# The second layer's down projection as seven products of sums of blocks, with tokens on the partitions, placed between the steps of the up projection

## The chip, the cores and the metric

The kernel runs on one core of one Trainium2 chip. The metric is the device time of one execution in microseconds. The kernel before was run three times: 2359.8, 2360.07 and 2360.8 us, a median of 2360.07 us. Engines are named as in the profile: PE multiplies matrices, PEld is its loading of weights, DVE, ACT and POOL work elementwise, SP issues most of the DMAs.

## What is computed

A decoder of two layers over 16 meta tokens and 256 tokens, with a residual stream of 2048 features, all in float32. The change touches the channel mixer of the second layer and the final norm behind it:

```python
def squared_relu_mlp(h, w_up, w_down):
    u = h @ w_up
    return jnp.square(jax.nn.relu(u)) @ w_down
...
        h = h + squared_relu_mlp(rms_norm(h, norm_mlp[layer]), w_up[layer], w_down[layer])
    return rms_norm(h, final_norm)[:, N_META:]
```

`w_up` is 2048 x 8192 and `w_down` 8192 x 2048 in each layer. The result has the 256 tokens alone, so in the second layer the meta tokens go into keys and values only.

## The kernel before

The residual `hT` lies with features on the partitions: 16 chunks of 128 features, 272 columns of tokens each. Every large product is a `gemm_group` (line 161): it computes 512 output features as four PSUM accumulators (`accs`) over 2048 input features, in four steps `kb` that each load 1 MB of weights (`raw`, line 185, on SP's queue, three buffers).

Products keep float32 precision by splitting each operand into two float32r parts: ACT writes the high part (`whi`, line 197), DVE subtracts it from the operand and so has the low part (`wlo`, line 198), in pieces of 128x1024. The activations are split likewise (`Split`, line 109). Three products make one: high by high, high by low, low by high. In the first layer they are three matmuls of 272 columns (lines 220 to 222). In the second layer (`pairs`) the first two are one matmul of 512 columns, since the high and low parts of 256 tokens lie side by side (line 217), and the third has 256 columns (line 218). The weights are the stationary operand, the activations the moving one.

`mlp` (line 444) goes over four quarters `f` of the 8192 hidden features: four groups of the up projection, whose results are scaled, rectified (lines 235 and 457), squared (line 459) and split (lines 460 and 461) into `u`, then four groups of the down projection, each adding its accumulators to `hT` (line 228). So in the second layer the stage has 1024 pairs of matmuls for the up projection and 1024 for the down projection. The final norm sums squares with small matmuls (line 594), takes the reciprocal root (lines 614 to 620), spreads it over the partitions (line 626) and scales and stores the result (lines 632 to 643).

PSUM has eight banks in two pools of four: `pacc` for the accumulators of `gemm_group` and `patt` for all else. The order of the instructions in each engine's queue is made by a planner, which estimates how long each one takes, from the order of the program; waits are put in by it too. In the kernel before POOL does little: masks at the start, small copies that pack keys, queries and values for the attention (lines 316 and 417), and two products at the end (line 641).

Of the kernel before, what the change touches and what calls it, by code (L numbers as in the profile page):

```python
# [15 lines left out]
P = 128  # L16
D = 2048
# [15 lines left out]
def yoco_kernel(ctx: ExitStack, tc: tile.TileContext, hT_in, gains, b_f, w_f, w_qkv0, w_o0, w_up, w_dn,  # L33
                w_kv, w_q1, w_o1, outT):
# [5 lines left out]
    align = ctx.enter_context(tc.tile_pool(name="align", bufs=1))  # L40
# [3 lines left out]
    att = ctx.enter_context(tc.tile_pool(name="att", bufs=2))  # L44
# [8 lines left out]
    bf_sb = const.tile([NC, 1], F32, name="bf_sb")  # L53
# [5 lines left out]
    for _ in range(7):  # L59
        nc.tensor.matmul(idle[:, :P], mean_w, mean_w, start=True, stop=True)  # L60
    ident = const.tile([P, P], F32, name="ident")
    make_identity(nc, ident)
    nones = const.tile([P, P], F32, name="nones")
    nc.vector.memset(nones, -1.0)
    nones_r = const.tile([P, P], F32R, name="nones_r")
    nc.vector.tensor_copy(nones_r, nones)

    ntri = const.tile([P, P], F32, name="ntri")
# [3 lines left out]
    ntri_r = const.tile([P, P], F32R, name="ntri_r")  # L72
# [3 lines left out]
    maskA = const.tile([P, 416], F32, name="maskA")  # L76
# [6 lines left out]
    maskM = const.tile([64, 4, 32], F32, name="maskM")  # L83
# [7 lines left out]
    maskB = const.tile([P, 400], F32, name="maskB")  # L91
# [6 lines left out]
    maskC = const.tile([64, 4, M], F32, name="maskC")  # L98
# [6 lines left out]
    pad = align.tile([P, 32], F32, name="pad")  # L105
# [55 lines left out]
    def gemm_group(wblk, sp, t0, evac, before={}, after={}, load_x=None, pairs=False, apart=()):  # L161
# [9 lines left out]
        for kb in range(4):  # L171
# [36 lines left out]
            for kc, m in order:  # L208
# [7 lines left out]
                if pairs and m not in apart:  # L216
# [6 lines left out]
                if last:  # L223
                    evac(m, [accs[m][:, :n]] + ([accs[m][:, n:]] if pairs and m not in apart else []))
# [34 lines left out]
    fq_sb = const.tile([P, 2, NC], F32, name="fq_sb")  # L259
    fqm_sb = const.tile([64, 4], F32, name="fqm_sb")  # L260
# [12 lines left out]
    def forget_gates(rstd):  # L273

        wf_hi, wf_lo = box["wf"]
        pf = patt.tile([P, 512], F32, tag="patt", name="pf")
        for k in range(NC):
            nc.tensor.matmul(pf[:NC, :T], wf_hi[:, k, :], xa.hi[:, k], start=k == 0, stop=False)
            nc.tensor.matmul(pf[:NC, :T], wf_hi[:, k, :], xa.lo[:, k], start=False, stop=False)
            nc.tensor.matmul(pf[:NC, :T], wf_lo[:, k, :], xa.hi[:, k], start=False, stop=k == NC - 1)  # L280
        fx = tmp.tile([P, T], F32, tag="relu", name="fx")[:NC]
# [43 lines left out]
    vz = const.tile([P, 4, P], F32, name="vz")  # L325
# [118 lines left out]
    def mlp(layer, xm, norm, t0, last_evac):  # L444
# [5 lines left out]
        for f in range(N_FF):  # L450
            u = Split(f"u{layer}_{f}", t0)
            for g in range(4):
                def evac(m, acc, g=g):
                    c = 4 * g + m
                    r = tmp.tile([P, T], F32, tag="relu", name=f"relu_{layer}_{f}_{c}")
                    u2 = tmp.tile([P, T], F32, tag="u2", name=f"u2_{layer}_{f}_{c}")
                    nc.vector.scalar_tensor_tensor(out=r[:, t0:], in0=total(acc, r[:, t0:]), scalar=0.0, in1=box["r"][:, t0:],
                                                   op0=ALU.max, op1=ALU.mult)
                    nc.scalar.activation(u2[:, t0:], r[:, t0:], AF.Square)
                    nc.scalar.activation(u.hi[:, c], u2[:, t0:], AF.Copy)  # L460
                    nc.vector.tensor_tensor(out=u.lo[:, c], in0=u2[:, t0:], in1=u.hi[:, c].bitcast(F32),
                                            op=ALU.subtract)
                gemm_group(w_up[layer, f, g], xm, t0, evac, {3: get_rstd} if f == g == 0 else {},
                           pairs=t0 == M)
            for g in range(4):
                def evac(m, acc, g=g):
                    residual_add(4 * g + m, acc, t0)
                    if f == N_FF - 1:
                        last_evac(4 * g + m)
                gemm_group(w_dn[layer, f, g], u, t0, evac, pairs=t0 == M,  # L470
                           apart=(3,) if layer == 1 and f == N_FF - 1 and g == 3 else ())
# [12 lines left out]
    mlp(0, xm, norm_m, 0, after_layer0)  # L484
# [104 lines left out]
    pms = patt.tile([P, 512], F32, tag="patt", name="pms_fin")  # L589
    box = {}  # L590

    def add_squares(src, first, last):
        for b in range(2):
            nc.tensor.matmul(pms[:, b:b + 1], src[:, M + b * P:M + (b + 1) * P], mean_w[:, 0:1],
                             start=first and b == 0, stop=last and b == 1)

    normf = Norm("fin", M)

    def last_evac(c):
        if c < NC - 4:  # L600
            normf.add(c)
        else:
            if c == NC - 4:
                add_squares(normf.acc, True, False)
            sq = tmp.tile([P, T], F32, tag="sq", name=f"sq_fin_{c}")
            nc.scalar.activation(sq[:, M:], hT[:, c, M:], AF.Square)
            add_squares(sq, False, c == NC - 1)
        if c < NC - 4:
            nc.scalar.activation(hT[:, c, M:], hT[:, c, M:], AF.Copy, scale=g_sb[:, G_FIN, c:c + 1])

    mlp(1, xm, norm_m, M, last_evac)
    fin = tmp.tile([P, 4, 2], F32, tag="fin", bufs=1, name="fin")
    a, y, t, rs = (fin[:, i, :] for i in range(4))
    nc.vector.tensor_scalar(a, pms[:, :2], EPS, None, op0=ALU.add)
# [80 lines left out]
```

## Time and profile before

| | |
|---|---|
| median of the runs | 2360.07 us |
| the profiled execution, its own time | 2360.31 us |
| its span (first to last instruction) | 2358.6 us |
| granted TensorE clock, mean | 0.998 |
| instructions | 39145 |
| bytes read from HBM over the span | 407.29 MB |
| DMA, mean rate over the span | 175 GB/s |

The span runs from the first instruction of the program to its last one; the execution's time holds 1.7 us more, which lie around it. An engine's busy time counts each moment once. A matmul's own duration is longer than the distance to the next one, because they are pipelined: what a matmul costs is read from how many start in a stretch of time. A DVE instruction too starts some 0.08 us before the one ahead of it has ended.

### The profile page before, as it was taken

The numbers are of one execution on the slowest core, as the hardware profiler recorded it, in microseconds if no ns is written. First come the engines' busy times: TensorE is split into PE (matmuls) and PEld (weight loads), VectorE is DVE, ScalarE is ACT, GpSimd is POOL, SyncE is SP. The second block draws the span as 40 slices with busy tenths as digits, with TensorE's granted clock in tenths as the row PEclk, the third lists the DMA queues.
The fourth block names the chain that finished last, engine by engine and source line by source line (L and its number), as shares of the span: only waits on it lengthen the run. The fifth ranks groups of instructions, "written<-read, shape, count | busy, mean of one in ns | idle before, by whom it ended". The sixth has DMA issues, their size and how long they took to land.

```text
span 2358.6 us, 39145 instructions
## 1 busy us (share of the span) xinstructions
PE 2344.8 (99%) x16512; PEld 2211.8 (94%) x16512; DVE 1343.1 (57%) x1916; ACT 1057.1 (45%) x1471; POOL 35.9 (2%) x64
## 2 busy tenths in 40 slices
PE   9999999999999999999999999999999999999998
PEld 9999999999999999999998999988888888888887
DVE  7565555655455455445566555566555655655665
ACT  5443344543344344344445444445543543543543
POOL 0000000000000000000000000000000000000000
PEclk9999999999999999999999999999999999999999
DMA  6444444554545455554545444445555555455453
GB/s 235 145 164 171 155 159 163 176 180 169 189 163 186 171 180 178 179 179 173 178 168 197 156 147 145 144 177 180 183 178 193 192 183 197 169 190 195 178 196 125
DMA packets 61039, 411.92 MB, mean 175 GB/s; under 512 B 7088, under 2 KB 10048, under 8 KB 12096
## 3 DMA queue, kind: packets, MB, share of 16 engines
q1 hardware_dynamic: 58976, 406.27, 48.5%
q8 instruction: 129, 2.11, 0.4%
q10 hardware_dynamic: 1888, 3.16, 0.4%
q14 instruction: 46, 0.38, 0.0%
HBM read 407.29 MB, written 2.11 MB: 174 GB/s over the span
## 4 chain that ended last, share of the span: by engine, by line
PE 99%; DVE 0%; ACT 0%; DMA 0%; issue 0%; DVEq 0%; SPq 0%; ACTq 0%
PE acc L217 25%; PE acc L220 19%; PE acc L221 19%; PE acc L222 19%; PE acc L218 13%; PE ps L365 0%; PE pza L542 0%; PE pv L307 0%; PE po L426 0%; PE po L427 0%; PE po L581 0%; PE po L582 0%; PE pzb L543 0%; PE po L428 0%; DMA g_sb<-gains 0%; ACT whi L197 0%
## 5 line engine op out<-in xcount | busy, mean ns | idle before, releaser
L198 DVE TENSOR_TENSOR wlo<-raw,whi 128x1024 fp32r<-128x1024 f32 (+1 forms) x771 | 932.5, 1220 | 761.5 <-ACT whi L197 758.2
L197 ACT ACTIVATE whi<-raw 128x1024 fp32r<-128x1024 f32 (+1 forms) x771 | 803.2, 1054 | 1072.4 <-PE acc L221 678.3
L217 PE MATMUL acc<-x_m,whi 128*128 128x512 f32 x1024 | 343.1, 394 | 0.5 <-DVE relu L235 0.5
L217 PE MATMUL acc<-x_u,whi 128*128 128x512 f32 x1008 | 337.9, 394 | 0.0
L220 PE MATMUL acc<-x_u,whi 128*128 128x272 f32 (+1 forms) x1040 | 297.7, 289 | 0.0
L221 PE MATMUL acc<-x_u,whi 128*128 128x272 f32 (+1 forms) x1040 | 294.8, 286 | 0.0
L220 PE MATMUL acc<-x_m,whi 128*128 128x272 f32 x1024 | 293.4, 289 | 0.0
L221 PE MATMUL acc<-x_m,whi 128*128 128x272 f32 x1024 | 290.4, 286 | 0.0
L222 PE MATMUL acc<-x_u,wlo 128*128 128x272 f32 (+1 forms) x1040 | 285.2, 284 | 0.0
L222 PE MATMUL acc<-x_m,wlo 128*128 128x272 f32 x1024 | 280.7, 284 | 0.0
L218 PE MATMUL acc<-x_m,wlo 128*128 128x256 f32 x1024 | 252.6, 282 | 0.0
L218 PE MATMUL acc<-x_u,wlo 128*128 128x256 f32 x1008 | 247.6, 281 | 0.0
L220 PE MATMUL acc<-x_a,whi 128*128 128x272 f32 x768 | 222.1, 294 | 0.7 <-ACT x_a L122 0.7
L221 PE MATMUL acc<-x_a,whi 128*128 128x272 f32 x768 | 221.0, 292 | 0.0
L217 PEld LDWEIGHTS acc<-x_m,whi 128*128 128x128 f32 x1024 | 185.0, 188 | 30.3 <-DVE relu L235 0.9
L222 PE MATMUL acc<-x_a,wlo 128*128 128x272 f32 x768 | 210.5, 287 | 0.0
L218 PEld LDWEIGHTS acc<-x_m,wlo 128*128 128x128 f32 x1024 | 192.3, 188 | 19.4 <-DVE wlo L198 4.6
L217 PEld LDWEIGHTS acc<-x_u,whi 128*128 128x128 f32 x1008 | 182.4, 188 | 29.7
L218 PEld LDWEIGHTS acc<-x_u,wlo 128*128 128x128 f32 x1008 | 189.3, 188 | 15.9 <-DVE wlo L198 1.6
L220 PEld LDWEIGHTS acc<-x_u,whi 128*128 128x128 f32 x1040 | 195.5, 188 | 0.2
L221 PEld LDWEIGHTS acc<-x_u,whi 128*128 128x128 f32 x1040 | 195.3, 188 | 0.1
L220 PEld LDWEIGHTS acc<-x_m,whi 128*128 128x128 f32 x1024 | 192.5, 188 | 0.0
(246 smaller groups left out, 3613.0 us busy)
## 6 DMA issues: line engine op xcount, KB each, us to landing
raw<-w_up SPq DMA_DIRECT2D x128, 1024.0 KB, 4.9
raw<-w_dn SPq DMA_DIRECT2D x128, 1024.0 KB, 4.9
raw<-w_qkv SPq DMA_DIRECT2D x45, 1024.0 KB, 4.8
raw<-w_o SPq DMA_DIRECT2D x32, 1024.0 KB, 4.8
raw<-w_kv SPq DMA_DIRECT2D x32, 1024.0 KB, 4.9
raw<-w_q SPq DMA_DIRECT2D x16, 1024.0 KB, 4.8
fk<-f_dram ACTq DMA_DIRECT2D x4, 544.0 KB, 5.2
raw<-w_qkv SPq DMA_DIRECT2D x4, 512.0 KB, 8.3
```

What stands on the lines that cost most here:

```text
L197: on_act = nc.scalar.activation(hp, src, AF.Copy)
L198: on_dve = nc.vector.tensor_tensor(out=lp, in0=src, in1=hp.bitcast(F32), op=ALU.subtract)
L217: nc.tensor.matmul(accs[m], wh, sp.both[:, k], start=first, stop=False)
L218: nc.tensor.matmul(accs[m][:, :n], wl, hi, start=False, stop=last)
L220: nc.tensor.matmul(accs[m][:, :n], wh, hi, start=first, stop=False)
L221: nc.tensor.matmul(accs[m][:, :n], wh, lo, start=False, stop=False)
L222: nc.tensor.matmul(accs[m][:, :n], wl, hi, start=False, stop=last)
```

## The change

The down projection of the second layer no longer goes through `gemm_group`. Tokens become the output's partitions: the result is held in `res`, 128 tokens by 2048 features for each half of the tokens, and the squared activations are now the stationary operand and the weights the moving one. `to_tokens` turns the residual round by 32 transposes, during the first block of the up projection.

The hidden features are taken in eight blocks `b` of 1024. For one block the activations are a matrix of 256 tokens by 1024 features, cut into 2x2 quarters, and so are the weights (512 features by 1024 outputs each quarter). The product of the two is computed by seven products of quarters or sums of quarters where the plain way takes eight. `build_forms` makes the seven forms of the activations for a block (four sums and the split of each, all on DVE and ACT). `down_block` goes over four pieces `n` of 256 columns of each half of the outputs, and over four steps `kp`: a step takes 128x256 of each quarter of the weights, makes four sums on POOL (`t`), splits three quarters and four sums on ACT and DVE (`hi`, `lo`: 128x768 and 128x1024), and issues 21 matmuls of 256 columns (`PRODUCTS`, three each) into the four banks of `patt`. After the fourth step the seven results are added to the four quarters of `res`, with two copies on ACT, five additions on DVE and six on POOL.

The weights are put into memory in this order on the host (`_quarters`), 1 MB for two steps. The steps of block b-1 are handed out behind the steps `kb` of the two up groups of block b by `SHARE`: none, 2, 2, 2, 2, 3, 3, 2. The last block runs by itself behind the last up group.

The final norm takes its sums of squares from ACT (`accum_out`) on `res`, the gain comes as a row spread over the partitions (`g_fin`), POOL multiplies three quarters of the last block's results by it, and the output goes out token by token. Smaller parts: the masks and other tiles of the attention move to a pool that is closed before the second layer's channel mixer; the matmuls ahead of the first load grow from 7 to 9; the products of the forget gates (`gate_products`) are issued ahead of the first norm's matmul, where they stood behind it; `mlp` becomes `mlp0` for the first layer alone, and `apart` goes.

```diff
-    for _ in range(7):
+    for _ in range(9):
...
-    def gemm_group(wblk, sp, t0, evac, before={}, after={}, load_x=None, pairs=False, apart=()):
+    def gemm_group(wblk, sp, t0, evac, before={}, after={}, load_x=None, pairs=False, behind=None):
...
+            if behind is not None:
+                behind(kb)
...
+            gate_products()
...
+    att_scope.close()
+    mlp = ctx.enter_context(tc.tile_pool(name="mlp", bufs=2))
+    NB = 8
+    res = mlp.tile([P, 2, D], F32, bufs=1, name="res")
+    uraw = hT[:, 0:8, :S]
+    usum = hT[:, 8:16, :S].rearrange("p (s a) (b t) -> p s a b t", a=2, b=2)
+    A11, A12, A22, S1, S2, S3, S4 = range(7)
+    B11, B21, B22, W5, T3, T2, T4 = range(7)
+    PRODUCTS = ((A11, B11, 0, 0), (S2, T2, 0, 1), (A12, B21, 1, 0), (S1, W5, 1, 1),
+                (S3, T3, 2, 0), (S4, B22, 2, 1), (A22, T4, 3, 0))
+    mbox = {}
+    def to_tokens(i, q):
+        pt = patt.tile([P, 512], F32, tag="patt", name=f"pt_res_{i}_{q}")
+        for c in range(4):
+            nc.tensor.transpose(pt[:, c * P:(c + 1) * P], hT[:, 4 * q + c, M + i * P:M + (i + 1) * P], ident)
+        nc.scalar.copy(res[:, i, 512 * q:512 * (q + 1)], pt)
+    def build_forms(b):
+        forms = xs.tile([P, 7, 2, 4, P], F32R, tag="x", name=f"forms_{b}")
+        half = {(i, j): uraw[:, 4 * j:4 * j + 4, i * P:(i + 1) * P] for i in range(2) for j in range(2)}
+        fold = lambda x: x.rearrange("p (a b) t -> p a b t", a=2)
+        a11, a12, a21, a22 = (fold(half[k]) for k in ((0, 0), (0, 1), (1, 0), (1, 1)))
+        def put(form, src):
+            hi, lo = forms[:, form, 0], forms[:, form, 1]
+            nc.scalar.activation(hi, src, AF.Copy)
+            nc.vector.tensor_tensor(out=lo, in0=src, in1=hi.bitcast(F32), op=ALU.subtract)
+        nc.vector.tensor_tensor(out=usum[:, 0], in0=a21, in1=a22, op=ALU.subtract)
+        nc.vector.tensor_tensor(out=usum[:, 1], in0=usum[:, 0], in1=a11, op=ALU.subtract)
+        nc.vector.tensor_tensor(out=usum[:, 2], in0=a11, in1=a21, op=ALU.subtract)
+        nc.vector.tensor_tensor(out=usum[:, 3], in0=a12, in1=usum[:, 1], op=ALU.add)
+        put(A11, half[0, 0])
+        put(A12, half[0, 1])
+        for k in range(2):
+            hi, lo = (forms[:, S1 + 2 * k:S1 + 2 * k + 2, h].rearrange("p s (a b) t -> p s a (b t)", a=2)
+                      for h in range(2))
+            src = hT[:, 8 + 4 * k:12 + 4 * k, :S].rearrange("p (s a) t -> p s a t", a=2)
+            nc.scalar.activation(hi, src, AF.Copy)
+            nc.vector.tensor_tensor(out=lo, in0=src, in1=hi.bitcast(F32), op=ALU.subtract)
+        put(A22, half[1, 1])
+        mbox["forms"] = forms
+    def down_block(b):
+        forms = mbox["forms"]
+        last = b == NB - 1
+        for n in range(4):
+            banks = [patt.tile([P, 2, 256], F32, tag="patt", name=f"m_{b}_{n}_{i}") for i in range(4)]
+            for kp in range(4):
+                if kp % 2 == 0:
+                    raws = wraw.tile([P, 2, 4, 256], F32, tag="raw", name=f"rawd_{b}_{n}_{kp}")
+                    nc.sync.dma_start(raws, w_dn1[b, n, kp // 2].rearrange("p (k q c) -> p k q c", k=2, q=4))
+                raw = raws[:, kp % 2]
+                b12, b11, b21, b22 = (raw[:, q] for q in range(4))
+                t = mlp.tile([P, 4, 256], F32, tag="sums", name=f"sums_{b}_{n}_{kp}")
+                nc.gpsimd.tensor_tensor(out=t[:, 1], in0=b22, in1=b12, op=ALU.add)
+                nc.gpsimd.tensor_tensor(out=t[:, 2], in0=t[:, 1], in1=b11, op=ALU.add)
+                nc.gpsimd.tensor_tensor(out=t[:, 0], in0=b11, in1=b12, op=ALU.add)
+                nc.gpsimd.tensor_tensor(out=t[:, 3], in0=t[:, 2], in1=b21, op=ALU.add)
+                hi = mlp.tile([P, 7, 256], F32R, tag="dhi", name=f"dhi_{b}_{n}_{kp}")
+                lo = mlp.tile([P, 7, 256], F32R, tag="dlo", name=f"dlo_{b}_{n}_{kp}")
+                for w0, w1, src in ((0, 3, raw[:, 1:4]), (3, 7, t)):
+                    nc.scalar.activation(hi[:, w0:w1], src, AF.Copy)
+                    nc.vector.tensor_tensor(out=lo[:, w0:w1], in0=src, in1=hi[:, w0:w1].bitcast(F32),
+                                            op=ALU.subtract)
+                for a, w, bank, h in PRODUCTS:
+                    m = banks[bank][:, h]
+                    nc.tensor.matmul(m, forms[:, a, 0, kp], hi[:, w], start=kp == 0 and h == 0, stop=False)
+                    nc.tensor.matmul(m, forms[:, a, 1, kp], hi[:, w], start=False, stop=False)
+                    nc.tensor.matmul(m, forms[:, a, 0, kp], lo[:, w], start=False,
+                                     stop=kp == 3 and (h == 1 or bank == 3))
+                if kp < 3:
+                    yield
+            c11, c12, c21, c22 = (res[:, i, 1024 * j + 256 * n:1024 * j + 256 * (n + 1)]
+                                  for i in range(2) for j in range(2))
+            (p1, p6), (p2, q5), (p7, q3), (q4, _) = ((x[:, 0], x[:, 1]) for x in banks)
+            ev = mlp.tile([P, 4, 256], F32, tag="ev", bufs=1, name=f"ev_{b}_{n}")
+            p1s, q5s, u2, u3 = (ev[:, k] for k in range(4))
+            late = nc.vector if last and n == 3 else nc.gpsimd
+            nc.scalar.copy(p1s, p1)
+            nc.vector.tensor_tensor(out=u2, in0=p6, in1=p1s, op=ALU.add)
+            nc.vector.tensor_tensor(out=c11, in0=p2, in1=c11, op=ALU.add)
+            nc.scalar.copy(q5s, q5)
+            nc.gpsimd.tensor_tensor(out=c11, in0=c11, in1=p1s, op=ALU.add)
+            nc.vector.tensor_tensor(out=u3, in0=p7, in1=u2, op=ALU.add)
+            nc.vector.tensor_tensor(out=c12, in0=q3, in1=c12, op=ALU.add)
+            nc.vector.tensor_tensor(out=c21, in0=q4, in1=c21, op=ALU.add)
+            nc.gpsimd.tensor_tensor(out=c12, in0=c12, in1=q5s, op=ALU.add)
+            nc.gpsimd.tensor_tensor(out=c12, in0=c12, in1=u2, op=ALU.subtract)
+            nc.gpsimd.tensor_tensor(out=c22, in0=c22, in1=q5s, op=ALU.add)
+            late.tensor_tensor(out=c22, in0=c22, in1=u3, op=ALU.subtract)
+            late.tensor_tensor(out=c21, in0=c21, in1=u3, op=ALU.add)
+            if last:
+                for i in range(2):
+                    for j in range(2):
+                        c = res[:, i, 1024 * j + 256 * n:1024 * j + 256 * (n + 1)]
+                        junk = tmp.tile([P, T], F32, tag="sq", name=f"junk_{n}_{i}_{j}")
+                        nc.scalar.activation(junk[:, :256], c, AF.Square,
+                                             accum_out=mbox["ssq"][:, i, 2 * n + j:2 * n + j + 1])
+                        if n < 3:
+                            nc.gpsimd.tensor_tensor(out=c, in0=c, in1=mbox["g_fin"][:, 1024 * j + 256 * n:
+                                                                                    1024 * j + 256 * (n + 1)],
+                                                    op=ALU.mult)
+            yield
+    def get_rstd2():
+        mbox["r"] = norm_m.finish()
+    SHARE = (0, 2, 2, 2, 2, 3, 3, 2)
+    for b in range(NB):
+        steps = down_block(b - 1) if b else iter(())
+        def start_down():
+            build_forms(b - 1)
+        for gg in range(2):
+            def evac(m, acc, gg=gg):
+                r = tmp.tile([P, T], F32, tag="relu", name=f"relu_1_{b}_{4 * gg + m}")[:, :S]
+                nc.vector.scalar_tensor_tensor(out=r, in0=total(acc, r), scalar=0.0, in1=mbox["r"][:, M:],
+                                               op0=ALU.max, op1=ALU.mult)
+                nc.scalar.activation(uraw[:, 4 * gg + m], r, AF.Square)
+            def behind(kb, gg=gg):
+                h = 4 * gg + kb
+                if b == 0:
+                    to_tokens(h % 2, h // 2)
+                for _ in range(SHARE[h]):
+                    next(steps, None)
+            before = {}
+            if gg == 0:
+                before = {0: start_down} if b else {3: get_rstd2}
+            gemm_group(w_up[1, b // 2, 2 * (b % 2) + gg], xm, M, evac, before, pairs=True, behind=behind)
+    g_fin = mbox["g_fin"] = xs.tile([P, D], F32, tag="x", name="g_fin")
+    nc.scalar.dma_start(g_fin, g_row.to_broadcast([P, D]))
+    ssq = mbox["ssq"] = tmp.tile([P, 2, 8], F32, tag="ssq", bufs=1, name="ssq_fin")
+    build_forms(NB - 1)
+    for _ in down_block(NB - 1):
+        pass
...
+    ms = t
+    nc.vector.tensor_reduce(out=ms, in_=ssq, op=ALU.add, axis=AX.X)
+    nc.vector.tensor_scalar(a, ms, 1.0 / D, EPS, op0=ALU.mult, op1=ALU.add)
...
+        for j in range(2):
+            c0 = 1024 * j
+            old = res[:, i, c0:c0 + 768]
+            if j == 0:
+                nc.vector.tensor_scalar(old, old, rs[:, i:i + 1], None, op0=ALU.mult)
+            else:
+                nc.scalar.activation(old, old, AF.Copy, scale=rs[:, i:i + 1])
+            (nc.sync if j == 0 else nc.scalar).dma_start(out[i, :, c0:c0 + 768], old)
+    for i in range(2):
+        for j in range(2):
+            c0 = 1024 * j + 768
+            new = res[:, i, c0:c0 + 256]
+            nc.vector.scalar_tensor_tensor(out=new, in0=new, scalar=rs[:, i:i + 1], in1=g_fin[:, c0:c0 + 256],
+                                           op0=ALU.mult, op1=ALU.mult)
+            nc.sync.dma_start(out[i, :, c0:c0 + 256], new)
...
+    q = w.reshape(8, 2, 2, 2, P, 2, 4, 256)
+    q = np.stack([q[:, 0, ..., 1, :, :], q[:, 0, ..., 0, :, :], q[:, 1, ..., 0, :, :], q[:, 1, ..., 1, :, :]])
+    return np.ascontiguousarray(q.transpose(1, 5, 2, 4, 3, 0, 6)).reshape(8, 4, 2, P, 2048)
```

More of the change, by code (lines that the diff above doesn't have):

```diff
@@ L32, in yoco_kernel @@
 @with_exitstack
-def yoco_kernel(ctx: ExitStack, tc: tile.TileContext, hT_in, gains, b_f, w_f, w_qkv0, w_o0, w_up, w_dn,
-                w_kv, w_q1, w_o1, outT):
+def yoco_kernel(ctx: ExitStack, tc: tile.TileContext, hT_in, gains, g_row, b_f, w_f, w_qkv0, w_o0, w_up,
+                w_dn0, w_dn1, w_kv, w_q1, w_o1, out):
     nc = tc.nc
@@ L215, in gemm_group @@
                 hi, lo = sp.hi[:, k], sp.lo[:, k]
-                if pairs and m not in apart:
+                if pairs:
                     nc.tensor.matmul(accs[m], wh, sp.both[:, k], start=first, stop=False)
@@ L442, in out_proj, with mlp0 @@
         return xm, norm
-    def mlp(layer, xm, norm, t0, last_evac):
+    def mlp0(xm, norm, last_evac):
         box = {}
@@ L586, in yoco_kernel @@
     xm, norm_m = out_proj(w_o1, ao, M, G_M1, "m1")
[L589 to L609, printed above, removed]
@@ L679 @@
         "w_up": np.stack([_blocks(w).reshape(4, 4, 4, P, 2048) for w in w_up]),
-        "w_dn": np.stack([[_blocks(w[i * D:(i + 1) * D]) for i in range(N_FF)] for w in w_down]),
+        "w_dn0": np.stack([_blocks(w_down[0][i * D:(i + 1) * D]) for i in range(N_FF)]),
+        "w_dn1": _quarters(w_down[1]),
         "w_kv": kv.transpose(1, 0, 2, 3, 4).reshape(8, 4, P, 2048),
```

94 lines of the change are left out of this document (36 added, 58 removed).

## The prediction

> **What bounds the kernel now.** First I read the page's busy times and the chain that ended last.
>
> ```profile
> PE 2344.8 (99%) x16512; PEld 2211.8 (94%) x16512; DVE 1343.1 (57%) x1916; ACT 1057.1 (45%) x1471; POOL 35.9 (2%) x64
> ...
> PE 99%; DVE 0%; ACT 0%; DMA 0%; issue 0%; DVEq 0%; SPq 0%; ACTq 0%
> ```
>
> PE is busy throughout and the chain of waits lies on it, so a change gains what it takes off PE, until another engine becomes the bound. The stage that changes is found from the rows of line 217 and the first matmul of the final norm.
>
> ```profile
> L217 PE MATMUL acc<-x_m,whi x1024: 388/392/505, 1622.2 to 2254.0; 128*128 128x512 f32 x171
> ```
> ```profile
> 2344.77 2.23 PE L594 MATMUL pms_fin<-mean_w,sq_fin 128*128 128x1 f32 x16
> ```
>
> From 1622.2 to 2344.8 us the second layer's channel mixer takes 722.6 us: 361 for each of its two projections. What a matmul costs, I take from how many fit in a stretch: the first row below has 272-column matmuls, each with its own weights, the second alternates 512 and 256 columns.
>
> ```profile
> 1090.00:1205.00 115.00, 115.00 (x927) 115.00 (x926) 65.31 (x88) 52.98 (x74) 0.00 (x0) 1.00 0.52 183
> ...
> 1726.00:1816.00 90.00, 90.00 (x516) 78.64 (x515) 49.47 (x64) 33.32 (x33) 0.00 (x0) 1.00 0.54 194
> ```
>
> 115/927 is 124 ns for 272 columns, 0.456 ns a column; 90/516 is 174 ns for 384 on average, 0.454. The time goes by columns, and a load of weights before each matmul is hidden at 272. A matmul of 256 columns is thus put at 117 ns.
>
> **The change on PE.** A step has 21 matmuls of 256 columns, 21 x 0.117 = 2.46 us; 128 steps (8 x 4 x 4) make 315 us in place of 361: 46 less, one eighth. The 32 transposes cost 32 x 0.155 = 5 us by the row of line 307 below (9.9 us busy for 64). PE's own work in the stage falls from 722.6 to 682 us.
>
> **What is put on DVE and POOL.** The prices come from these rows: groups, then single lines, then the timeline, where "x2" is two in a row.
>
> ```profile
> L307 PE MATMUL pv<-ident,vT 128*128 128x128 f32 x64 | 9.9, 276 | 0.0
> L198 DVE TENSOR_TENSOR wlo<-raw,whi 128x1024 fp32r<-128x1024 f32 (+1 forms) x771 | 932.5, 1220 | 761.5 <-ACT whi L197 758.2 <-PE acc L218 2.5
> L197 ACT ACTIVATE whi<-raw 128x1024 fp32r<-128x1024 f32 (+1 forms) x771 | 803.2, 1054 | 1072.4 <-PE acc L221 678.3 <-PE acc L217 383.9 <-issue 4.0
> L637 DVE TENSOR_TENSOR ob<-hT,pr_fin 128x512 f32<-128x512 f32 x4 | 2.5, 679 | 0.0
> L641 POOL TENSOR_TENSOR ob<-hT,pr_sb 128x512 f32<-128x512 f32 x2 | 2.5, 1273 | 822.3 <-ACT pr_sb L631 822.3
> L234 ACT COPY relu<-acc 128x256 f32<-128x256 f32 x64 | 23.1, 362 | 41.4 <-PE acc L218 40.1
> ```
> ```profile
> L457 DVE SCALAR_TENSOR_TENSOR relu<-relu,rstd_m x64: 414/418/425, 1646.0 to 2258.9; 128x256 f32<-128x256 f32 x64
> ```
> ```profile
> 1239.98 2.35 DVE L198 TENSOR_TENSOR wlo<-raw,whi 128x1024 fp32r<-128x1024 f32 x2
> ...
> 2350.89 2.51 POOL L641 TENSOR_TENSOR ob<-hT,pr_sb 128x512 f32<-128x512 f32 x2 [822.26 <-ACT pr_sb L631]
> 2351.16 2.47 DVE L637 TENSOR_TENSOR ob<-hT,pr_fin 128x512 f32<-128x512 f32 x4
> ```
>
> On DVE, 1024 columns cost 2.35 - 1.22 = 1.13 us start to start. 512 columns: the four of line 637 take 2.47 us, less 0.68 for the last, over three: 0.60. The line through both is 1.035 ns a column and 0.07 us fixed, so 768 cost 0.87 and 256 cost 0.34. On POOL two additions of 512 columns take 2.51 us, less 1.27 for the last: 1.24 start to start, and one of 256 is put at 0.62, half of it. No row shows that width; more than 1.24, or less than a copy of 128 columns below (0.28 for each of two), it can't be.
>
> A step therefore has 0.87 + 1.13 = 2.0 us of splits on DVE and 4 x 0.62 = 2.5 us of sums on POOL, beside 2.46 on PE. Taken engine by engine this fits: between steps of the up projection PE has 361/128 = 2.8 us more for each. The ACT copies of a step are 1.05 us and three quarters of it, which also fits.
>
> **The two engines do not run beside each other.** These rows are POOL's copies for the attention (line 316), and DVE in the same microseconds.
>
> ```profile
> 38.19 0.24 POOL L316 COPY pk_qm<-qT 128x64 f32<-128x64 f32 x1 [32.40 <-DVE qT L335]
> 93.14 1.22 POOL L316 COPY pk_vm<-vT 128x128 f32<-128x128 f32 x1 [19.11 <-DVE vT L339]
> 122.66 1.10 POOL L316 COPY pk_qm<-qT 128x64 f32<-128x64 f32 x1 [22.93 <-DVE qT L335]
> 156.09 0.56 POOL L316 COPY pk_sm<-s 128x128 f32<-128x128 f32 x2 [32.34 <-DVE s L375]
> ```
> ```profile
> 92.64 0.44 DVE L339 TENSOR_TENSOR vT<-acc,rstd_a 128x272 f32<-128x272 f32 x1 [1.05 <-PE acc L222]
> 92.99 2.44 DVE L198 TENSOR_TENSOR wlo<-raw,whi 128x1024 fp32r<-128x1024 f32 x2
> ```
>
> The same copy of 64 columns takes 0.24 us or 1.10, that of 128 columns 0.29 (two in 0.56) or 1.22. The long one began at 93.14, 0.15 us into a split of line 198 (92.99), and ended at 94.36, 0.15 us after that split ended at 94.21: it stood still for the whole split. The next split then waited for it: the pair takes 2.44 us where an undisturbed pair takes 2.35. The splits read two tensors from SBUF, and so does every sum of the change; DVE and POOL take turns at something that one of them holds for a whole instruction. The additions of line 641 took 1.27 us each beside those of line 637, whose second input is in PSUM: there nothing is shared.
>
> The Trainium skill's page "SBUF — State Buffer", section "Who interferes with whom", says the same for more than these rows show: a DVE instruction with two SBUF inputs contends with any GpSimd instruction that reads SBUF, and whichever began first holds the shared read port to its end. By that rule each sum on POOL holds DVE for its whole stream; the row of the copies alone gives less, the low bound below. Its page "GPSIMD Engine Reference", section "3.1 Elementwise — side-by-side cycle accounting", has 4497 ns for an addition of 2048 float32 columns; an estimate from that page is 0.56 us for 256, and the stage's sum by it would be 43 us shorter than mine.
>
> **The sum.** Turns at this one door, in us. DVE, two SBUF inputs: splits of the steps 128 x 2.0 = 256; the forms, per block four sums and three splits of 512 columns at 0.60 and two splits of 1024 at 1.13, 6.5, times 8 = 52; splits of the up projection 128 x 1.13 = 145; the scaling of line 457, 64 x 0.34 = 22. Together 475. (The additions that read PSUM, lines 228 and 235 now and five per piece later, do not count.) POOL: 512 sums; 6 x 32 - 2 = 190 additions of results; 12 products with the gain: 714 x 0.62 = 443. Together 918. The first up block has no steps beside it: an eighth of 145 and 22, 21 us, lies inside its own 361/8 = 45 us on PE, to which the transposes add 5. The stage takes 45 + 5 + 918 - 21 = 947 us where it takes 722.6: **224 us more**.
>
> Two corrections are of opposite sign. POOL's fixed part can hide: the copy of 0.29 us kept DVE only 0.09, so 0.2 of each addition may not hold the door; a 256-column addition then holds (1.24 - 0.2)/2 = 0.52, 714 x 0.1 = 71 less, and DVE's fixed 0.07 us on 520 instructions is 36 less: the low bound is 840, +117. The high bound adds stretches in which neither is at the door: behind the last sum of a piece come ACT's copy (1.05) and PE's step (2.46) before POOL can add the results, 3.5 us x 32 = 112 if nothing is put between: 1059, +336. They cancel, so I keep +224.
>
> **The smaller parts.** These rows bear on them.
>
> ```profile
> 1.12 3.35 PE L60 MATMUL idle<-mean_w 128*128 128x128 f32 x14 [1.12 <-DVE mean_w L56]
> 5.18 1.27 PE L220 MATMUL acc<-x_a,whi 128*128 128x272 f32 x4 [0.71 <-ACT x_a L122]
> ...
> 32.28 0.73 PE L145 MATMUL pms_a<-ssq_a,mean_w 128*128 128x272 f32 x2 [0.94 <-DVE ssq_a L140]
> ```
> ```profile
> raw<-w_dn SPq DMA_DIRECT2D x128, 1024.0 KB, 4.9
> ```
>
> Two more matmuls at the start are four records of 0.24 us, about 1 us against a gap of 0.71: nothing to +0.3. The gate products fill the 0.94 us before the norm's matmul: -1 at most. DMAs: the same 64 loads of 1 MB on SP's queue, at the same buffers, each landing in 4.9 us beside 5 us of PE for two steps; they hide now (DMA share 0.54 above) and more so in a longer stage. Behind the last matmul now lie 13.8 us (2344.8 to 2358.6); later the norm needs no matmuls, but four DVE additions, squares, the root and eight stores follow the last product: taken as equal, within 4 either way.
>
> Span: 2358.6 + 224 - 1 = 2582; with the 1.7 us around it the execution takes 2583, and the profiled 2360.31 lies 0.24 above the median of the runs. Rounded: **2580 us**.
>
> **Rival 1, PE stays the bound.** If a two-input sum on POOL does not hold DVE, the door is open and the 682 us of PE count. No row shows such a sum beside a two-input DVE instruction, only one-input copies; those speak against it. The point from which it decides: the stage is no longer than now if a sum holds at most (722.6 - 50 - 454)/714 = 0.31 us. Even then the last block has no up steps as cover: POOL's 64 sums, 22 additions and 12 products take 61 us beside 39 of PE, +22, and its forms (6.5) stand bare: 682 + 29 = 711, -12: **2348 us**.
>
> **Rival 2, slower without the door: four banks.** Each piece takes all four buffers of `patt`, so the next piece's first product waits until DVE has read them: five additions of 0.34 and a copy of 0.36 (line 234), 2.1 us one after the other. On rival 1's 2348, three of four piece ends have an up step behind them (5.6 us on PE); bare, 8 x 2.1 = 17, **2365 us**; with every one bare, 32 x 2.1 = 67, 2415.
>
> **Rival 3, the order doesn't do what it says.** If the planner leaves POOL's additions of a piece ahead of the next piece's sums and sets no up step between, each piece is a chain: 0.42 + 6 x 0.62 + 4 x 0.62 + 1.05 + 1.22 = 8.9 us, times 32 = 285 on 682: 967, **2605 us**, with POOL waiting rather than held; with the door on top, over 2700.
>
> **How the numbers follow.** The forecast, the door, has 0.68, with its own range 2475 to 2695; rival 3 has 0.07, half of it above 2690; rival 2 0.08, mostly slower; rival 1 0.17. A measurement of this kernel tells 0.2% (5 us) from no change. Faster by more: rival 1 without its slowest cases, 0.16; within: 0.04; slower: 0.80. To leave out no more than two in ten the range must reach rival 1's price: 2340 to 2695.
>
> **What would show it.** Right: in the second layer's channel mixer POOL's sums of 256 columns last well over 0.62 us, the splits beside them are stretched beyond 1.22, PE is busy some 70 to 75% of the stretch and waits for DVE's low parts. Wrong: sums at 0.62 and splits at 1.22 side by side with PE at 97% (rival 1); PE waiting for DVE's reads of PSUM (rival 2); POOL idle until results arrive (rival 3). A matmul of 256 columns above 0.125 us, or a tail that isn't 10 to 18 us long, would break smaller steps.

## The result, and the profile after

| | before | changed | |
|---|---|---|---|
| median, us | 2360.05 (4 runs) | 2588.15 (2587.16 to 2589.6, 4 runs) | ratio 1.0966, 95% interval 1.0947 to 1.0985 |
| span of the profiled execution, us | 2358.6 | 2587.3 | +228.7 |
| granted clock, mean | 0.998 | 0.968 | |

The page of the changed kernel: busy times, three rows of the 40 slices (here 64.7 us each), and the chain that ended last.

```profile
PE 2396.4 (93%) x17144; PEld 2275.9 (88%) x17144; DVE 1656.5 (64%) x2075; ACT 1178.7 (46%) x1652; POOL 882.1 (34%) x776
...
DVE  6555556554544544556655556687888879888764
...
POOL 0000000000000000000000000189999999999997
PEclk9999999999999999999999999999999989899977
...
POOL 9%; DVE 2%; issue 1%; PE 0%; ACT 0%; DMA 0%; POOLq 0%; DVEq 0%; ACTq 0%
```

POOL was idle and is busy from the 26th slice on. The chain, which lay on PE, is now followed back over some 12% of the span only (to 2268 us: the last block and nearly all of the two before it), and 9 of them are on POOL. The granted clock is below nine tenths in the 33rd, the 35th and the last two slices, where PE works in stretches with gaps.

The stage again by the matmuls of the up projection (line 218 in the changed kernel) and the last of each product (line 674).

```profile
L218 PE MATMUL acc<-x_m,whi x1024: 387/392/629, 1627.8 to 2461.3; 128*128 128x512 f32 x171
```
```profile
L674 PE MATMUL m<-dlo,forms x896: 274/283/582, 1676.9 to 2572.4; 128*128 128x256 f32 x180
```

It starts at 1627.8 us and ends at 2572.4: 944.6 us, where 722.6 stood before. The steps begin at 1676.9; the seven blocks from there to the last up matmul at 2461.3 take 784.4 us, 112 each, and the last block, alone, 111. The same 450 us seen engine by engine, before and after (columns: PE, PEld, DVE, ACT, POOL busy, granted clock, DMA share, GB/s):

```profile
1800.00:2250.00 450.00, 450.00 (x2558) 389.97 (x2557) 263.60 (x365) 206.45 (x292) 0.00 (x0) 1.00 0.52 187
```
```profile
1800.00:2250.00 450.00, 376.93 (x2332) 336.20 (x2331) 374.58 (x367) 221.72 (x308) 424.13 (x351) 0.93 0.42 148
```

DMA went down, ACT hardly moved, DVE is busy 375 of 450 us and POOL 424. The lower clock is not what bounds: at 0.93, the 84.6 us that PE needs for a block (45.2 for the up projection, 39.4 for the steps) would be 91, an estimate, and a block takes 112. How they stand to each other is in the groups of the new instructions, and in the timelines of the two engines over the same microseconds.

```profile
L668 DVE TENSOR_TENSOR dlo<-sums,dhi 128x1024 fp32r<-128x1024 f32 x128 | 191.2, 1493 | 161.5 <-ACT dhi L667 161.5
...
L661 POOL TENSOR_TENSOR sums<-sums,rawd 128x256 f32<-128x256 f32 x128 | 182.6, 1427 | 0.0
L668 DVE TENSOR_TENSOR dlo<-rawd,dhi 128x768 fp32r<-128x768 f32 x128 | 169.7, 1326 | 16.1 <-ACT dhi L667 16.1
L662 POOL TENSOR_TENSOR sums<-rawd 128x256 f32<-128x256 f32 x128 | 167.3, 1307 | 0.0
L660 POOL TENSOR_TENSOR sums<-rawd 128x256 f32<-128x256 f32 x128 | 154.9, 1210 | 187.2 <-DMA rawd<-w_dn 176.4 <-DVE dlo L668 10.8
...
L663 POOL TENSOR_TENSOR sums<-sums,rawd 128x256 f32<-128x256 f32 x128 | 134.9, 1054 | 6.0
```
```profile
1803.62 1.75 DVE L199 TENSOR_TENSOR wlo<-raw,whi 128x1024 fp32r<-128x1024 f32 x1
...
1806.44 1.76 DVE L642 TENSOR_TENSOR forms<-hT,forms 128x1024 fp32r<-128x1024 f32 x1
1808.12 1.76 DVE L668 TENSOR_TENSOR dlo<-sums,dhi 128x1024 fp32r<-128x1024 f32 x1
1809.80 1.76 DVE L199 TENSOR_TENSOR wlo<-raw,whi 128x1024 fp32r<-128x1024 f32 x1
```
```profile
1798.43 0.74 POOL L689 TENSOR_TENSOR res<-res,ev 128x256 f32<-128x256 f32 x1
1799.13 0.74 POOL L695 TENSOR_TENSOR res<-res,ev 128x256 f32<-128x256 f32 x1
...
1804.25 1.72 POOL L663 TENSOR_TENSOR sums<-sums,rawd 128x256 f32<-128x256 f32 x1
...
1807.08 1.72 POOL L660 TENSOR_TENSOR sums<-rawd 128x256 f32<-128x256 f32 x1
1808.75 1.72 POOL L662 TENSOR_TENSOR sums<-rawd 128x256 f32<-128x256 f32 x1
```

Left to itself POOL starts an addition of 256 columns every 0.70 us (1798.43 to 1799.13, each lasting 0.74). Beside DVE's splits it starts one every 1.67, and so does DVE: 1806.44, 1808.12, 1809.80 on DVE against 1807.08, 1808.75 on POOL. That is one split (1.13) and one addition (0.54) in turn, each instruction's time stretched over the other's. In the groups POOL's sums last 1.05 to 1.43 us on average and the splits 1.33 and 1.49, where 0.95 and 1.22 would do.

What PE waits for is, above all, the high parts of the sums: ACT copies them once POOL has made them. The low parts from DVE come behind that.

```profile
L672 PE MATMUL m<-dhi,forms 128*128 128x256 f32 x896 | 272.2, 310 | 107.2 <-ACT dhi L667 79.3
...
L674 PE MATMUL m<-dlo,forms 128*128 128x256 f32 x896 | 264.8, 312 | 19.0 <-DVE dlo L668 18.2
...
L667 ACT ACTIVATE dhi<-sums 128x1024 fp32r<-128x1024 f32 x128 | 135.2, 1057 | 314.9 <-POOL sums L663 314.9
```

### The profile page after: what moved, and what is told of

Its sections match the earlier page's. It is cut to its first block, busy times and chain, and to the rows that moved or that the text cites. A ratio compares the mean times of both kernels' runs of the same rounds, so it can differ in the third digit from the quotient of the medians.

```text
span 2587.3 us, 41408 instructions
## 1 busy us (share of the span) xinstructions
PE 2396.4 (93%) x17144; PEld 2275.9 (88%) x17144; DVE 1656.5 (64%) x2075; ACT 1178.7 (46%) x1652; POOL 882.1 (34%) x776
## 5 line engine op out<-in xcount | busy, mean ns | idle before, releaser
L198 ACT ACTIVATE whi<-raw 128x1024 fp32r<-128x1024 f32 (+1 forms) x643 | 671.2, 1053 | 812.8 <-PE acc L222 675.9
L672 PE MATMUL m<-dhi,forms 128*128 128x256 f32 x896 | 272.2, 310 | 107.2 <-ACT dhi L667 79.3
L672 PEld LDWEIGHTS m<-dhi,forms 128*128 128x128 f32 x896 | 187.1, 210 | 124.0 <-ACT dhi L667 86.0
L668 DVE TENSOR_TENSOR dlo<-sums,dhi 128x1024 fp32r<-128x1024 f32 x128 | 191.2, 1493 | 161.5 <-ACT dhi L667 161.5
L221 PE MATMUL acc<-x_u,whi 128*128 128x272 f32 x1024 | 293.2, 289 | 0.0
L222 PE MATMUL acc<-x_u,whi 128*128 128x272 f32 x1024 | 290.3, 286 | 0.0
L673 PE MATMUL m<-dhi,forms 128*128 128x256 f32 x896 | 267.3, 303 | 16.6 <-DVE forms L642 12.0
L674 PE MATMUL m<-dlo,forms 128*128 128x256 f32 x896 | 264.8, 312 | 19.0 <-DVE dlo L668 18.2
L223 PE MATMUL acc<-x_u,wlo 128*128 128x272 f32 x1024 | 280.7, 284 | 0.0
L667 ACT ACTIVATE dhi<-sums 128x1024 fp32r<-128x1024 f32 x128 | 135.2, 1057 | 314.9 <-POOL sums L663 314.9
L218 PEld LDWEIGHTS acc<-x_m,whi 128*128 128x128 f32 x1024 | 195.1, 194 | 48.6 <-issue 10.0
L660 POOL TENSOR_TENSOR sums<-rawd 128x256 f32<-128x256 f32 x128 | 154.9, 1210 | 187.2 <-DMA rawd<-w_dn 176.4
```

Of the source, the lines that this page charges most:

```text
L198: on_act = nc.scalar.activation(hp, src, AF.Copy)
L218: nc.tensor.matmul(accs[m], wh, sp.both[:, k], start=first, stop=False)
L221: nc.tensor.matmul(accs[m][:, :n], wh, hi, start=first, stop=False)
L222: nc.tensor.matmul(accs[m][:, :n], wh, lo, start=False, stop=False)
L223: nc.tensor.matmul(accs[m][:, :n], wl, hi, start=False, stop=last)
L660: nc.gpsimd.tensor_tensor(out=t[:, 1], in0=b22, in1=b12, op=ALU.add)
```

## The experiments

**Which one is it: turns, a slow POOL, or a chain?** Three readings give about the same time for the changed kernel: DVE and POOL take turns (the door); an addition on POOL simply takes 1.2 us; or each piece is a chain of results, additions, sums, copy and split. Two kernels leave out one side of the meeting each, one keeps POOL's time but not its reads, and one has DVE do the sums.

`no_low` leaves out DVE's splits in the steps:

```diff
-                    nc.vector.tensor_tensor(out=lo[:, w0:w1], in0=src, in1=hi[:, w0:w1].bitcast(F32),
-                                            op=ALU.subtract)
...
-                    nc.tensor.matmul(m, forms[:, a, 0, kp], lo[:, w], start=False,
+                    nc.tensor.matmul(m, forms[:, a, 0, kp], zlo, start=False,
```

> The low parts of the weights in the steps of the down projection are left out on DVE (the third matmul of each product reads a tile of zeros in their place); POOL's sums, ACT's copies and all matmuls stay. Door (DVE and POOL take turns where both read two tensors from SBUF): the turns fall by 256 us to 662, the stage is 45 + 5 + 662 - 21 = 691 us, hardly more than PE's 682, so 2330 to 2355 us, and a sum on POOL falls from 1.2 to 1.4 us to 0.6 to 0.9. Rival 'POOL is slow by itself' (a sum takes its 1.2 us whatever DVE does): POOL's 714 x 1.2 = 857 us stay, about 2540. Rival 'chain' (each piece waits for results, additions, sums, copy, split in a row): 32 x 1.22 less, about 2550.

Measured: 2405.3 us (one run; before beside it 2360.35). Two of its groups, and its stage:

```profile
L666 POOL TENSOR_TENSOR sums<-rawd 128x256 f32<-128x256 f32 x128 | 113.3, 886 | 0.0
...
L665 POOL TENSOR_TENSOR sums<-sums,rawd 128x256 f32<-128x256 f32 x128 | 110.9, 873 | 0.0
```
```profile
L218 PE MATMUL acc<-x_m,whi x1024: 388/392/633, 1629.3 to 2304.9; 128*128 128x512 f32 x171
```
```profile
L675 PE MATMUL m<-zlo,forms x896: 274/283/416, 1677.9 to 2387.9; 128*128 128x256 f32 x180
```

POOL's four sums (lines 664 to 667 here, 660 to 663 before) take 0.87, 0.87, 0.89 and 0.97 us on average where they took 1.21, 1.43, 1.31 and 1.05, and 183 us are gone: POOL is not slow by itself, and a chain that lost only 1.22 us a piece would have kept 2550. The forecast of 2330 to 2355 was too low, though. From the first up matmul to the last product it takes 2387.9 - 1629.3 = 759 us in place of 691. The price of an addition explains little of the 68: 474 of the 714 lasted under 0.75 us (counted in the trace), and with 0.70 for them and 0.54 for the rest they come to 461 us in place of 443. The forecast spread one sum of turns over the whole stage. But the seven blocks can't go below PE's 84.6 us each and took 89.6, and the last block has no up steps beside it and took 83.0, where POOL's 98 additions alone are 69 at 0.70. Why a block takes 5 us more than PE needs was not taken apart.

`no_sums` leaves out POOL's four sums (the second split reads the four quarters themselves):

```diff
-                nc.gpsimd.tensor_tensor(out=t[:, 1], in0=b22, in1=b12, op=ALU.add)
...
-                for w0, w1, src in ((0, 3, raw[:, 1:4]), (3, 7, t)):
+                for w0, w1, src in ((0, 3, raw[:, 1:4]), (3, 7, raw)):
```

> POOL's four sums of each step are left out (the four split forms are the four quarters themselves); all splits, copies and matmuls stay, and POOL's additions of results. Door: turns 475 + 125 = 600, below PE's 682, so PE bounds: 2315 to 2340 us, splits of 1024 columns at 1.2 to 1.3 us. POOL slow by itself: the same time, so this run does not tell it from the door. Chain: 32 x 2.5 = 80 less, about 2510.

Measured: 2362.58 us (one run).

```profile
L218 PE MATMUL acc<-x_m,whi x1024: 388/392/629, 1628.4 to 2272.9; 128*128 128x512 f32 x171
```
```profile
L669 PE MATMUL m<-dlo,forms x896: 274/283/419, 1677.1 to 2345.7; 128*128 128x256 f32 x180
```

From the first step to the last up matmul (1677.1 to 2272.9) seven blocks take 596 us, 85.1 each: PE's 84.6. What misses the forecast is the last block, 72.8 us against 39 of PE: the splits, copies and POOL's 34 instructions have no up steps beside them, and DVE is busy 56 of these 73 us.

`sums_memset` keeps POOL's time, the place of its instructions in the program and those who wait for them, but it writes only:

```diff
-                nc.gpsimd.tensor_tensor(out=t[:, 1], in0=b22, in1=b12, op=ALU.add)
...
+                for i in range(4):
+                    nc.gpsimd.memset(tf[:, 352 * (i % 2):352 * (i % 2) + 672], 0.5)
```

> POOL's four sums of each step become four fills of 672 columns of the same tile, about as long as a sum alone (0.6 us by the fills at the start of the program), so POOL's time, its order and who waits for it stay; it only reads nothing. Door: the fills take no turns, 600 us of turns, PE bounds with the last block's POOL bare: 2325 to 2355 us, fills at 0.6 us, splits at 1.2 to 1.3. Chain: unchanged, 2570 to 2600. POOL slow by itself: does not say, 2325 to 2355.

Measured: 2375.4 us (one run). Its fills and the splits of the filled tile (shortest, median, longest in ns), and its stage:

```profile
L662 POOL MEMSET sums<- x512: 651/661/675, 1546.6 to 2353.0; 128x672 f32 x171
```
```profile
L667 DVE TENSOR_TENSOR dlo<-sums,dhi x128: 1205/1225/1789, 1552.0 to 2354.7; 128x1024 fp32r<-128x1024 f32 x128
```
```profile
L218 PE MATMUL acc<-x_m,whi x1024: 388/392/505, 1626.5 to 2267.2; 128*128 128x512 f32 x171
```
```profile
L673 PE MATMUL m<-dlo,forms x896: 278/283/580, 1675.1 to 2358.8; 128*128 128x256 f32 x180
```

512 fills of 0.66 us run beside the splits, whose median is 1.225 us again: undisturbed. From 1675.1 to 2267.2 us the seven blocks take 84.6 us each, PE's own pace. Time on POOL and order alone cost 2375.4 - 2362.6 = 13 us over `no_sums`, all of it in the last block (2358.8 - 2267.2 = 91.6 us); reading on POOL costs the other 213. The chain theory, which had 2570 to 2600, falls with this. Two differences remain. A fill does not wait for the weights to land, and a sum does; in the changed kernel POOL's waits for weights come to some 30 us behind 1700 us of the span. And the planner puts POOL's additions of results at other places between the fills than between the sums. Against the chain speaks the changed kernel itself, too: in its stage POOL waits for results of the products only once, 1.5 us. The Trainium skill's page "SBUF — State Buffer", section "Who interferes with whom", has it that a DVE instruction with two SBUF inputs contends with a GpSimd instruction that reads SBUF and not with one that only writes; this run agrees.

`sums_dve` moves the four sums to DVE and leaves nothing out:

```diff
-                nc.gpsimd.tensor_tensor(out=t[:, 1], in0=b22, in1=b12, op=ALU.add)
+                nc.vector.tensor_tensor(out=t[:, 1], in0=b22, in1=b12, op=ALU.add)
```

> The four sums of each step go from POOL to DVE, 0.34 us each start to start, nothing left out. Door: turns 475 + 174 + 125 = 774 in place of 918, stage 803 us: 2440, up to 2500 since DVE's own queue has 725 us of instructions and waits for POOL's additions too. POOL slow by itself: POOL is off the path, DVE's 725 us in a stage of some 755: 2395. Chain: 32 x 4 x 0.28 = 36 less, 2550.

Measured: 2495.66 us (one run), at the upper end of what the door gave: 92 us are won by having the same additions done by the other of the two engines, 0.34 us each in place of a turn of 0.54 to 0.70. From 1800 to 2250 us DVE is busy 446 of 450 us, so that its own queue sets the pace there.

**The gate products.** The stage begins 5.6 us later than before. Ahead of it, PE's timeline of the changed kernel shows the first norm's matmul and the next wait:

```profile
35.69 0.62 PE L146 MATMUL pms_a<-ssq_a,mean_w 128*128 128x272 f32 x2
...
41.34 0.57 PE L221 MATMUL acc<-x_a,whi 128*128 128x272 f32 x1 [3.54 <-DVE qT L342]
```

The norm's matmul stood at 32.28 us before. `gates_back` puts the products behind it again:

```diff
-            gate_products()
             box["rstd"] = norm.finish()
...
+        gate_products()
         pf = box["pf"]
```

> The changed kernel with the products of the forget gates put back behind the first norm's matmul. In the profile of after the norm's matmul stands at 35.7 us (before: 32.3), PE then waits 3.5 us for results scaled by that norm, and the second layer's channel mixer starts at 1627.8 us (before: 1622.2). Theory: the gate products, ahead of the norm, delay it by their own 6 us and cost 4 us: the mixer starts 4 us earlier and the kernel takes 2584. Rival: the masks' new places or the two more matmuls at the start cost them: no change, 2588.

Measured: 2582.51 us (2581.97 to 2583.04, 2 runs).

```profile
L218 PE MATMUL acc<-x_m,whi x1024: 387/392/630, 1624.7 to 2455.1; 128*128 128x512 f32 x171
```

The stage starts 3.1 us earlier, and 5.6 us come back in all; the norm's matmul is at 33.19 us, and PE's wait of 3.54 us behind it is gone. Filling a gap of 0.94 us with 6 us of matmuls (48 of them) put the norm, which everything behind it waits for, later. The other 2.7 us lie in the stage (941.9 us in place of 944.6), whose code is the same in both, and are about as much as the runs of the changed kernel lie apart (2.4 us). The 2.5 us by which the stage still starts later than before were not taken apart.

**A version that stays under the door.** Turns are a sum, so they can be budgeted per block. Of each block's four pieces, some go by seven products and the rest the plain way: eight products with matmuls of 512 columns, one split of 1024, no sums. The last block is all plain, and its forms are made while the last two steps of the block before run.

```diff
+    SEVEN = lambda b, n: b < 7 and n % 2 == 0
...
+                if not SEVEN(b, n):
+                    nc.scalar.activation(hi[:, :4], raw, AF.Copy)
+                    nc.vector.tensor_tensor(out=lo[:, :4], in0=raw, in1=hi[:, :4].bitcast(F32), op=ALU.subtract)
+                    for i in range(2):
+                        for j, a in enumerate(((A12, A11), (A22, A21))[i]):
+                            w = slice(2 * j, 2 * j + 2)
+                            m = banks[i]
+                            nc.tensor.matmul(m, forms[:, a, 0, kp], hi[:, w], start=kp == j == 0, stop=False)
+                            nc.tensor.matmul(m, forms[:, a, 1, kp], hi[:, w], start=False, stop=False)
+                            nc.tensor.matmul(m, forms[:, a, 0, kp], lo[:, w], start=False, stop=kp == 3 and j == 1)
```

`half_pool` has two of four pieces by seven products with POOL's sums and additions, `quarter_pool` one of four, `half_dve` two of four with POOL's sums and additions of results on DVE; `three_dve` three of four, `plain_tok` none.

> A version that may beat both: tokens on the partitions, the gate products as before; of the four pieces of each block two go by seven products with POOL's sums, two the plain way (eight products, 512-column matmuls, one split of 1024 and no sums), the last block all plain, its forms covered by the last two steps of the block before. Per block, door (a POOL addition takes 0.54 us of it, as splits of 1.22 us that meet one last 1.76 in the runs so far): DVE 53, POOL 44 x 0.54 = 24, together 77 beside PE's 45 + 20 + 22 = 87: PE bounds. Stage 48 + 7 x 87 + 45 = 702 in place of 723, 2340 us, up to 2360 where turns fall at a bad place. If the door were no limit of the sum but each meeting cost PE (rival: waits, not turns), half the meetings of after keep half of its loss: about 2460.

> half_pool with one piece of four by seven products. PE 45 + 10 + 34 = 89 a block, door about 60: 48 + 7 x 89 + 45 = 716, 2352 us. If turns still bound half_pool, this one is the faster of the two.

> half_pool with the sums and the additions of results on DVE, none on POOL. DVE has 53 + 8 x 1.36 + 2 x 11 x 0.34 + 5 = 76 us a block in one queue beside PE's 87: 2340 us, at most 2355; better than half_pool if meetings at the door cost more than DVE's extra time, worse if DVE's one queue is late for PE.

> half_dve with no piece by seven products: tokens on the partitions, weights the moving operand, steps between those of the up projection, all the plain way. If half_dve's 17 us come from the products saved, this one has PE's full 45 + 45 us a block: 48 + 7 x 90 + 45 = 723, 2362 us. If they come from the layout or from the placing of the steps, it keeps them: 2345.

> half_dve with three of four pieces by seven products. PE 45 + 30 + 11 = 86 us a block, DVE 88 us in one queue (12 x 3.3 + 4.5 for the splits and sums, 15 for results, 28 for the rest). If the bound is DVE's sum, this is where it passes PE: about 2350, not faster than half_dve; if DVE's sum were no limit, PE alone would give 7 us less than half_dve, 2337.

| kernel | median, us | ratio to before | 95% interval |
|---|---|---|---|
| half_pool | 2362.5 (10 runs) | 1.0010 | 1.0001 to 1.0019 |
| quarter_pool | 2362.75 (8 runs) | 1.0009 | 0.9999 to 1.0019 |
| half_dve | 2343.86 (4 runs) | 0.9928 | 0.9912 to 0.9945 |
| plain_tok | 2351.41 (5 runs) | 0.9962 | 0.9947 to 0.9977 |
| three_dve | 2385.98 (3 runs) | 1.0109 | 1.0089 to 1.0128 |

The same 450 us of the stage in `half_pool`, `half_dve`, `plain_tok` and `three_dve`, in this order:

```profile
1800.00:2250.00 450.00, 437.18 (x2581) 385.09 (x2582) 369.40 (x399) 242.28 (x327) 250.34 (x220) 1.00 0.52 186
```
```profile
1800.00:2250.00 450.00, 449.04 (x2677) 399.15 (x2677) 399.75 (x641) 253.12 (x338) 0.00 (x0) 1.00 0.55 194
```
```profile
1800.00:2250.00 450.00, 450.00 (x2279) 382.18 (x2278) 263.74 (x305) 205.56 (x265) 0.00 (x0) 1.00 0.53 190
```
```profile
1800.00:2250.00 450.00, 427.23 (x2683) 381.27 (x2683) 427.78 (x744) 255.59 (x352) 0.00 (x0) 1.00 0.50 182
```

`half_dve` is faster than both kernels, 16 to 17 us under the one before: PE is busy 449 of 450 us and DVE 400. With three pieces of four DVE reaches 428 of 450 and PE drops to 427: the bound has passed to DVE, and it is slower than before, 2386 where 2350 was forecast. `half_pool` misses its forecast by 22 us: a sum of turns below PE's time is not enough, since POOL's 220 instructions in the window take 250 us, 1.14 each, and stretch splits that PE waits for (PE is busy 437 of 450 us). `quarter_pool`, with half as many meetings and one piece fewer by seven products, comes out the same, where 2352 was forecast.

Of the gain of `half_dve` less than half comes from seven products. `plain_tok`, without any, is 9 us under before, not equal as expected. Its matmuls follow each other more closely; the first and the last of ten in a row:

```profile
1899.70 0.39 PE L673 MATMUL m<-dhi,forms 128*128 128x512 f32 x1
...
1901.74 0.39 PE L673 MATMUL m<-dhi,forms 128*128 128x512 f32 x1
```

Nine distances in 2.04 us are 227 ns for 512 columns, 0.443 ns a column, where the pairs of 512 and 256 columns took 0.454: 2.4% of the down projection's 361 us is 8.7 us, about what was measured. That is a sum and not a test: the stage is 8.0 us shorter in the profile (714.6 us), transposes included, and no run changes only which operand is the moving one. Seven products add 7.5 us on top.

## Why the prediction was right

**The time.** 2580 was forecast and 2588 measured. The stage was put at 947 us and took 944.6; 5.6 us came ahead of it where -1 was expected, and 1.1 behind it (2587.3 - 2572.4 = 14.9 against 13.8) where none was.

**The door** was the right mechanism: `sums_memset` and `no_low` open it from either side, and the changed kernel's timelines show the turns. Of the forecast's 947 us, 50 are the first up block and 99 the turns of the last block (39 on DVE, 98 additions at 0.62 on POOL); the other 798 are 114 for each of seven blocks, against 112 measured.

**The price of an addition**, 0.62 us, was half a measured one of 512 columns. It is 0.70 alone and 0.54 in turns, so the estimate of 0.56 is near the latter only. Of POOL's 714 additions, 267 lasted under 0.75 us (counted in the trace) and are taken as alone, and a mean of 0.63 x 0.54 + 0.37 x 0.70 = 0.60 is close to the 0.62 by a mix, not by the halving. That is luck.

**The two corrections** that were let cancel do cancel, but not in their sizes: 107 us were put on one side and 112 on the other. With 0.60 in place of 0.62 the sum is 932 us, 14 less, and some 12 us of waits are left, mostly in the last block. There the turns are 39 us of DVE and 98 x 0.60 of POOL, 98, and it took 111. That they cancel is luck too: one addition and one split of 1024 columns in turn take 1.67 us, between the 1.75 of the sum and the 1.58 of the low bound (0.52 and 1.06), and the 0.70 of the additions that met nobody made up for it; the stretches in which neither is at the door came to about a tenth of what was put on them.

**Rival 1**, PE as the bound with the sums still on POOL, is what `sums_memset` shows in the seven blocks, at PE's 84.6 us. Its time is 2375, not 2348: the last block was put at 61 us by POOL alone and 6.5 for its forms, and took 91.6, and even `no_sums`, which has 34 of POOL's 98 instructions there, took 72.8. Rival 2's banks are there but small: by the waits of the changed kernel's profile PE waits some 15 us of the stage for the additions and copies that read the products. Rival 3's chain is not seen: POOL's waits for results are the 1.5 us above, and `sums_memset` keeps what the chain is made of.

**What was wrong** is the step on the gate products, "-1 at most": it looked at the gap that they fill and not at the norm behind them; `gates_back` shows 3 us of it at the start of the stage and 5.6 in all. Two of the signs named were wrong too. PE waits first for the high parts from ACT (79 us), which wait for POOL's sums, and only 18 us for DVE's low parts, though DVE was to be what holds it. And PE's busy share is not 70 to 75%: 377 of 450 us is 84%. A matmul of 256 columns lasts 0.28 us and costs 0.12, so that its duration reaches into the gap behind it, and with the clock at 0.93 durations grew (those of the first matmuls of the up projection from 394 to 403 ns on average).

## What to carry to other kernels

Before work goes to an idle POOL, add up what both engines read from SBUF in pairs: POOL's two-input instructions and DVE's two-input instructions are one queue for most of the time, and an addition is cheaper on DVE (0.34 us) than its turn on POOL (0.54 to 0.70). Fewer multiplications on the bound engine pay only as far as the engines that prepare the operands have time to spare: here two pieces of four, not four. A matrix product that ends a chain for everything behind it (a norm) is not to be moved behind fillers that are longer than the gap.

## What was not expected

The turns are not always one by one. In the stretch below POOL's addition, which takes 0.73 us alone, lasted 4.84 us, while six instructions of DVE with two SBUF inputs ran back to back at their undisturbed pace; another one lasted 7.16 us.

```profile
1792.94 4.84 POOL L662 TENSOR_TENSOR sums<-rawd 128x256 f32<-128x256 f32 x1
```
```profile
1792.95 0.69 DVE L629 TENSOR_TENSOR forms<-hT,forms 128x512 fp32r<-128x512 f32 x1
1793.55 0.69 DVE L631 TENSOR_TENSOR hT<-hT 128x512 f32<-128x512 f32 x1
1794.15 1.29 DVE L629 TENSOR_TENSOR forms<-hT,forms 128x512 fp32r<-128x512 f32 x2
1795.36 1.23 DVE L199 TENSOR_TENSOR wlo<-raw,whi 128x1024 fp32r<-128x1024 f32 x1
1796.49 0.69 DVE L632 TENSOR_TENSOR hT<-hT 128x512 f32<-128x512 f32 x1
```

Elsewhere POOL got in between two such instructions that follow each other without a gap. What decides it, no run here tells. It is not rare: in `sums_memset` six of the seven blocks have one addition of results that lasts 6.33 to 6.34 us, in `no_sums` one lasted 12.69 us and in `sums_dve` one 15.96. Each of these ended 0.6 us after DVE's row of instructions with two SBUF inputs had ended. So the rule that the prediction quotes, that whichever began first holds the port to its end, is not all of it: here POOL waited through many instructions of DVE, not one.
